# Rotary half-embedding: splitting the first load 4 + 12 rows and issuing tile 2's second half at a point of tile 1's arithmetic

## The chip, the cores and the metric

One core of one Trainium2 chip. The metric is the device time of one execution in microseconds; medians are over the executions of a run. There is only one core, so there are no other cores or dies to compare with; the granted clock was 1.0.

## The reference

`x` is 16 x 512 x 16 x 64 in fp32 (33.5 MB). The first half of the last axis is rotated with tables of cosines and sines, one row per position; the second half is copied.

```
x1, x2 = x[..., :32], x[..., 32:]
first  = x1[..., :16] * cos - x1[..., 16:] * sin      # cos, sin: first 16 columns, by position
second = x1[..., :16] * sin + x1[..., 16:] * cos
out    = concatenate([first, second, x2], axis=-1)
```

Every byte is read once and written once, 67.1 MB in all.

## The kernel before

Four tiles of 128 partitions x 16 rows (64 KB per partition, 8.4 MB each) go through three slots in SBUF. The rotation is in place on VectorE (DVE), eight rows at a time.

```python
ring = const_pool.tile([P, NS, K, H, D], fp32)         # NS = 3 slots, K = 16 rows, KC = 8, KM = 13
...
nc.gpsimd.dma_start(out=spread[:, 0, 0], in_=cosf)     # the two tables, on GpSimd's queue
nc.gpsimd.dma_start(out=spread[:, 0, 1], in_=sinf)
load(0)                                                # loads and stores: the sync engine's queue
load(1)
load(2, 0, KC)                                         # tile 2, first half
...                                                    # tables spread to all partitions
rotate(0, 0, KC)                                       # four VectorE instructions each
rotate(0, KC, K)
store(0)
load(2, KC, K)                                         # tile 2, second half, right behind store 0
load(3)                                                # slot of tile 0: waits until store 0 has landed
rotate(1, 0, KC)
rotate(1, KC, K)
behind_loads = store(1)                                # held until rotate(2, KC, KM) is done
rotate(2, 0, KC)
near = rotate(2, KC, KM)
rotate(2, KM, K)
store(2, queue=nc.gpsimd)
...
rotate(3, 0, KC)
rotate(3, KC, K)
store(3)
```

The sync engine works through its list in order: a transfer that has to wait holds up those written after it.

Of the kernel before, what the change touches and what calls it, by code (L numbers as in the profile page):

```python
# [1 line left out]

# [4 lines left out]


@with_exitstack
def kernel(  # L10
    ctx: ExitStack,
    tc: tile.TileContext,
    x: bass.AP,
    cos: bass.AP,
    sin: bass.AP,
    out: bass.AP,
):
    nc = tc.nc
    fp32 = mybir.dt.float32
    P = 128  # L20
    B, S, H, D = x.shape
    Q = D // 4
    HF = D // 2



    K = 16
    T = B * S // (P * K)
    PB = S // K
    REP = P // PB  # L30
    R = H * D
    NS = 3
    KC = K // 2
    KM = 13

    xf = x.rearrange("b s h d -> (b s h d)").rearrange("(t p f) -> t p f", t=T, p=P)
    of = out.rearrange("b s h d -> (b s h d)").rearrange("(t p f) -> t p f", t=T, p=P)
    cosf = cos.rearrange("(p k) j -> p (k j)", k=K)
    sinf = sin.rearrange("(p k) j -> p (k j)", k=K)

    const_pool = ctx.enter_context(tc.tile_pool(name="const", bufs=1))
    b_pool = ctx.enter_context(tc.tile_pool(name="bp", bufs=1, space=bass.MemoryType.PSUM))


    ring = const_pool.tile([P, NS, K, H, D], fp32)
    stage = const_pool.tile([P, 2, K, HF], fp32)
    spun = const_pool.tile([P, 2 * K, Q], fp32)
    packed = const_pool.tile([PB, 2 * K, Q], fp32)
    table = const_pool.tile([P, 2, K, 2, Q], fp32)

    def rows(t, lo, hi):
        return ring[:, t % NS, lo:hi].rearrange("p k h d -> p (k h d)")

    def load(t, lo=0, hi=K):
        return nc.sync.dma_start(out=rows(t, lo, hi), in_=xf[t, :, lo * R : hi * R])

    def store(t, lo=0, hi=K, queue=nc.sync):
        return queue.dma_start(out=of[t, :, lo * R : hi * R], in_=rows(t, lo, hi))  # L58


    nc.vector.memset(stage[:, :, :, 0:Q], 0.0)  # L61
    spread = stage.rearrange("(j b) t k i -> j b t (k i)", b=REP)
    nc.gpsimd.dma_start(out=spread[:, 0, 0], in_=cosf)  # L63
    nc.gpsimd.dma_start(out=spread[:, 0, 1], in_=sinf)  # L64
    load(0)
    load(1)
    load(2, 0, KC)




    PQ = PB // REP
    nc.vector.stream_shuffle(  # L73
        out=spun[:],
        in_=stage.rearrange("p t k j -> p (t k) j")[:, :, 0:Q],
        mask=[j % PQ * REP for j in range(PB)],
    )
    for q in reversed(range(REP)):
        n = PQ * (q + 1)
        nc.vector.tensor_copy(out=packed[0:n], in_=spun[q * PB : q * PB + n])  # L80

    for r in range(REP):
        nc.vector.tensor_copy(  # L83
            out=table[r * PB : (r + 1) * PB].rearrange("p t k c j -> p (t k) c j"),
            in_=packed.unsqueeze(2).to_broadcast((PB, 2 * K, 2, Q)),
        )
    C = table[:, 0].rearrange("p k c j -> p k (c j)")
    Sn = table[:, 1].rearrange("p k c j -> p k (c j)")

    def rotate(t, lo, hi):  # L90
        x1 = ring[:, t % NS, lo:hi, :, 0:HF]
        c = C[:, lo:hi].unsqueeze(2).to_broadcast((P, hi - lo, H, HF))
        s = Sn[:, lo:hi].unsqueeze(2).to_broadcast((P, hi - lo, H, HF))
        b_full = b_pool.tile([P, KC, H, HF], fp32, name="b_t")
        b_t = b_full[:, 0 : hi - lo]
        nc.vector.tensor_mul(out=b_t, in0=x1, in1=s)  # L96
        nc.vector.tensor_mul(out=x1, in0=x1, in1=c)  # L97
        nc.vector.tensor_sub(  # L98
            out=x1[:, :, :, 0:Q], in0=x1[:, :, :, 0:Q], in1=b_t[:, :, :, Q:HF]
        )  # L100
        return nc.vector.tensor_add(  # L101
            out=x1[:, :, :, Q:HF], in0=x1[:, :, :, Q:HF], in1=b_t[:, :, :, 0:Q]
        )

    rotate(0, 0, KC)
    rotate(0, KC, K)
    store(0)
    load(2, KC, K)
    load(3)
    rotate(1, 0, KC)  # L110
    rotate(1, KC, K)
    behind_loads = store(1)
    rotate(2, 0, KC)
    near = rotate(2, KC, KM)
    rotate(2, KM, K)
    store(2, queue=nc.gpsimd)

    tc.add_manual_dep(
        behind_loads.ins,
        near.ins.name,  # L120
        mybir.DependencyInfo(mybir.DependencyClass.Sync, mybir.DependencyReason.DATA),
        reason="the store follows the loads at the DMA engines",
    )
    rotate(3, 0, KC)
    rotate(3, KC, K)
    store(3)


# [1 line left out]
_INS = ['x', 'cos', 'sin']  # L130
_OUTS = [((16, 512, 16, 64), 'float32')]


# [23 lines left out]
```

## Time and profile before

| | before |
|---|---|
| time, median of the first 3 executions | 161.46 us (161.22 to 161.59) |
| span of the profiled execution | 159.5 us |
| bytes moved | 67.24 MB |
| VectorE busy | 112.9 us, 71% |
| DMA queues, share of 16 engines | 85.7% + 12.4% |
| first packet, last packet's end | 1.74 us, 158.2 us |

A profile of a kernel like this is read from the transfers, not from the engines: the DMA row and the queue table say that the sixteen DMA engines are at work for 98% of the span, and the trace's packet records (one start, duration and size per packet) say how well they work.

### The profile page before, as it was taken

The page shows a single profiled execution, that of the slowest core. Times are in us where ns is not written, and L with a number is a line of the kernel's source. Part 1 is how long each engine was busy: PE and PEld are TensorE (multiplying, and loading weights), DVE is VectorE, ACT ScalarE, POOL GpSimd, SP SyncE. Part 2 cuts the span into 40 slices and gives each one's busy share as a digit, 9 for nine tenths or more (in the row PEclk, how much of TensorE's full clock was granted, in tenths as well). Part 3 has the DMA queues.
Part 4 walks back from the last instruction along what each step waited for, and adds up shares of the span by engine and source line. Part 5 has one row for each costly group of instructions (what it writes and reads, how often), then busy time and mean ns, then how long its engine had stood idle before and what let it go on. Part 6 is the DMA issues. An engine that isn't in the chain of part 4 may idle for free.

```text
span 159.5 us, 115 instructions
## 1 busy us (share of the span) xinstructions
DVE 112.9 (71%) x47; POOL 1.9 (1%) x7
## 2 busy tenths in 40 slices
DVE  1000959999999999999999999999999990000000
POOL 3000000000000000000000000010000000000000
DMA  7969979899699699699996996996996996998966
GB/s 263 542 263 542 444 345 526 362 427 526 271 493 551 263 526 526 263 395 427 493 526 263 526 526 263 526 526 263 526 526 263 526 510 279 526 427 362 526 263 263
DMA packets 1360, 67.24 MB, mean 422 GB/s; under 512 B 176, under 2 KB 176, under 8 KB 208
## 3 DMA queue, kind: packets, MB, share of 16 engines
q1 hardware_dynamic: 1152, 58.72, 85.7%
q0 software_dynamic: 208, 8.52, 12.4%
HBM read 33.69 MB, written 33.55 MB: 422 GB/s over the span
## 4 chain that ended last, share of the span: by engine, by line
DVE 61%; DMA 14%; issue 5%; DVEq 1%
DVE b_t L96 22%; DVE ring L97 22%; DMA ring<-in_x_dram 14%; DVE ring L101 10%; DVE ring L98 7%; DVEq L152 1%; DVEq L96 0%
## 5 line engine op out<-in xcount | busy, mean ns | idle before, releaser
L96 DVE TENSOR_TENSOR b_t<-ring,table 128x4096 f32<-128x4096 f32 (+2 forms) x9 | 35.6, 3959 | 2.1 <-DMA ring<-in_x_dram 1.9
L97 DVE TENSOR_TENSOR ring<-ring,table 128x4096 f32<-128x4096 f32 (+2 forms) x9 | 35.6, 3950 | 0.3
L98 DVE TENSOR_TENSOR ring<-ring,b_t 128x2048 f32<-128x2048 f32 (+2 forms) x9 | 18.4, 2050 | 0.3
L101 DVE TENSOR_TENSOR ring<-ring,b_t 128x2048 f32<-128x2048 f32 (+2 forms) x9 | 18.4, 2043 | 0.0
L73 DVE LOAD_MASK_SELECT spun<-stage x1 | 0.0, 14 | 14.4 <-DMA stage<-in_sin_dram 14.4
L83 DVE COPY table<-packed 32x1024 f32<-32x1024 f32 x4 | 2.7, 684 | 0.1
L58 POOL DMA_DIRECT2D out_dram<-ring x1 | 0.6, 559 | 101.7 <-DVE ring L101 101.7
L80 DVE COPY packed<-spun 32x512 f32<-32x512 f32 (+3 forms) x4 | 1.7, 416 | 0.1
L61 DVE MEMSET stage<- 128x512 f32 x1 | 0.5, 485 | 0.9 <-PEq L141 0.9
L73 DVE STREAM_SHUFFLE spun<-stage 128x512 f32<-128x512 f32 x1 | 0.7, 722 | 0.0
L63 POOL DMA_DIRECT2D stage<-in_cos_dram x1 | 0.6, 642 | 1.3 <-DVE stage L61 1.3
L64 POOL DMA_DIRECT2D stage<-in_sin_dram x1 | 0.5, 532 | 0.0
L141 POOL MEMSET const-bfloat16-1.0<- 128x1 bf16 x1 | 0.1, 101 | 0.0
L141 POOL MEMSET const-float32-0.0<- 128x1 f32 x1 | 0.1, 98 | 0.2 <-issue 0.2
L141 POOL MEMSET const-float32-1.0<- 128x1 f32 x1 | 0.1, 98 | 0.0
L141 POOL MEMSET const-uint8-127<- 128x1 uint8 x1 | 0.1, 98 | 0.0
## 6 DMA issues: line engine op xcount, KB each, us to landing
ring<-in_x_dram SPq DMA_DIRECT2D x2, 4096.0 KB, 40.7
stage<-in_cos_dram POOLq DMA_DIRECT2D x1, 64.0 KB, 8.9
stage<-in_sin_dram POOLq DMA_DIRECT2D x1, 64.0 KB, 13.3
ring<-in_x_dram SPq DMA_DIRECT2D x3, 28.9
out_dram<-ring SPq DMA_DIRECT2D x3, 27.4
out_dram<-ring POOLq DMA_DIRECT2D x1, 39.5
```

The costliest lines, as they stand in the source:

```text
L58: return queue.dma_start(out=of[t, :, lo * R : hi * R], in_=rows(t, lo, hi))
L61: nc.vector.memset(stage[:, :, :, 0:Q], 0.0)
L63: nc.gpsimd.dma_start(out=spread[:, 0, 0], in_=cosf)
L64: nc.gpsimd.dma_start(out=spread[:, 0, 1], in_=sinf)
L73: nc.vector.stream_shuffle(out=spun[:], in_=stage.rearrange("p t k j -> p (t k) j")[:, :, 0:Q], mask=[j % PQ * REP for j in range(PB)],)
L80: nc.vector.tensor_copy(out=packed[0:n], in_=spun[q * PB : q * PB + n])
L83: nc.vector.tensor_copy(out=table[r * PB : (r + 1) * PB].rearrange("p t k c j -> p (t k) c j"), in_=packed.unsqueeze(2).to_broadcast((PB, ...
L96: nc.vector.tensor_mul(out=b_t, in0=x1, in1=s)
L97: nc.vector.tensor_mul(out=x1, in0=x1, in1=c)
L98: nc.vector.tensor_sub(out=x1[:, :, :, 0:Q], in0=x1[:, :, :, 0:Q], in1=b_t[:, :, :, Q:HF])
L101: return nc.vector.tensor_add(out=x1[:, :, :, Q:HF], in0=x1[:, :, :, Q:HF], in1=b_t[:, :, :, 0:Q])
L152: with _tile.TileContext(nc) as tc:
```

## The change

Its intent, by the text of the change: let the first rows come in as a small transfer of their own, and issue tile 2's second half "near the end of the one in front of it", as was done before for store 1 only.

```diff
-    load(0)
+    load(0, 0, KC // 2)
+    load(0, KC // 2, K)
     load(1)
     load(2, 0, KC)
...
     store(0)
-    load(2, KC, K)
+    rest = load(2, KC, K)
     load(3)
     rotate(1, 0, KC)
-    rotate(1, KC, K)
+    behind(rest, rotate(1, KC, K)[0])       # [0]: the first multiplication of that rotation
```

`rotate` now returns its first and last instruction, and `behind(transfer, point)` adds the dependence that store 1 had already. Nothing else moves.

More of the change, by code (lines that the diff above doesn't have):

```diff
@@ L95, in rotate @@
         b_t = b_full[:, 0 : hi - lo]
-        nc.vector.tensor_mul(out=b_t, in0=x1, in1=s)
+        begun = nc.vector.tensor_mul(out=b_t, in0=x1, in1=s)
         nc.vector.tensor_mul(out=x1, in0=x1, in1=c)
@@ L100, in rotate, with behind @@
         )
-        return nc.vector.tensor_add(
+        done = nc.vector.tensor_add(
             out=x1[:, :, :, Q:HF], in0=x1[:, :, :, Q:HF], in1=b_t[:, :, :, 0:Q]
+        )
+        return begun, done
+    def behind(transfer, point):
+        tc.add_manual_dep(
+            transfer.ins,
+            point.ins.name,
+            mybir.DependencyInfo(
+                mybir.DependencyClass.Sync, mybir.DependencyReason.DATA
+            ),
+            reason="issue the transfer near the end of the one in front of it",
         )
@@ L107 @@
     store(0)
-    load(2, KC, K)
+    rest = load(2, KC, K)
     load(3)
     rotate(1, 0, KC)
-    rotate(1, KC, K)
-    behind_loads = store(1)
+    behind(rest, rotate(1, KC, K)[0])
+    last = store(1)
     rotate(2, 0, KC)
-    near = rotate(2, KC, KM)
+    behind(last, rotate(2, KC, KM)[1])
     rotate(2, KM, K)
     store(2, queue=nc.gpsimd)
-    tc.add_manual_dep(
-        behind_loads.ins,
-        near.ins.name,
-        mybir.DependencyInfo(mybir.DependencyClass.Sync, mybir.DependencyReason.DATA),
-        reason="the store follows the loads at the DMA engines",
-    )
     rotate(3, 0, KC)
```

## The prediction

> **What bounds the kernel now.** I read the page first: the engines' busy shares, the DMA row of the forty slices, the queue table.
>
> ```profile
> DVE 112.9 (71%) x47; POOL 1.9 (1%) x7
> ...
> DMA  7969979899699699699996996996996996998966
> ...
> DMA packets 1360, 67.24 MB, mean 422 GB/s; under 512 B 176, under 2 KB 176, under 8 KB 208
> ...
> q1 hardware_dynamic: 1152, 58.72, 85.7%
> q0 software_dynamic: 208, 8.52, 12.4%
> ```
>
> VectorE (DVE) is busy for 71% of the span; the two DMA queues together for 85.7 + 12.4 = 98.1% of what sixteen engines could be. So the transfers bound the kernel. The 9-6-9 ripple is no idle time: a slice is 4 us, a packet is 64 KB and takes 2.4 us, and a packet is booked in one slice. Wider stretches, cut at the events of the queue, smooth it (columns: length, VectorE, GpSimd, clock, DMA share, GB/s):
>
> ```profile
> 0.00:1.74 1.74, 0.48 (x1) 0.24 (x5) 1.00 0.00 0
> ...
> 51.03:71.25 20.22, 20.08 (x6) 0.00 (x0) 1.00 1.03 439
> 71.25:99.85 28.60, 28.32 (x12) 0.00 (x0) 1.00 0.98 423
> 99.85:131.20 31.35, 31.04 (x12) 0.56 (x1) 1.00 1.00 435
> 131.20:158.20 27.00, 0.00 (x0) 0.00 (x0) 1.00 0.99 427
> 158.20:159.47 1.27, 0.00 (x0) 0.00 (x0) 1.00 0.00 0
> ```
>
> Nothing moves in the first 1.74 us and the last 1.27 us; between them the rate hardly leaves 430 GB/s, even after VectorE has finished at 131.2.
>
> The page's chain of waits says "DVE 61%; DMA 14%". That is a trap: it ends at the instruction that released the last store, and does not see that this store then stood in line behind another. So I went one level down, to the trace's packet records (start, duration, bytes), sorted by start into waves of sixteen, one packet per engine. They show one queue without a gap: 896 packets of 64 KB (56 waves, 2.418 us each at the median), 256 of 32 KB (16 waves of 1.213 us) and 32 table packets of 4 KB (2 waves of 0.159 us). At that pace: 56 x 2.418 + 16 x 1.213 + 2 x 0.159 = 155.1 us. From first packet to last end they took 158.22 - 1.74 = 156.5 us. **Only 1.3 us of 159.5 is lost inside the stream.** I find it in these places:
> - Wave 0, the first packets of all: 2.886 to 3.452 us each, mean 3.18, so about **0.75 us** over the pace. The engines start spread over 0.43 us.
> - Wave 31, the last packets of the first store, just ahead of tile 2's second half: those that began first took up to 3.318 us, those that began last 2.418. The latest end of the wave comes 81.73 - 78.93 = 2.80 us after that of the wave before, so about **0.38 us** over the pace.
> - The rest is some 5 ns per wave where stores run, and the spread at start and end.
>
> Last, the instruction timeline and the waits of the issuing queue:
>
> ```profile
> 0.74 1.33 SPq L55 DMA_DIRECT2D ring<-in_x_dram  x3
> ...
> 15.78 0.01 DVE L73 LOAD_MASK_SELECT spun<-stage  x1 [14.38 <-DMA stage<-in_sin_dram]
> ...
> 22.99 4.43 DVE L96 TENSOR_TENSOR b_t<-ring,table 128x4096 f32<-128x4096 f32 x1 [1.85 <-DMA ring<-in_x_dram]
> ...
> 49.87 0.35 SPq L58 DMA_DIRECT2D out_dram<-ring  x1
> ...
> 50.26 21.82 SPq L55 DMA_DIRECT2D ring<-in_x_dram  x2
> ```
>
> VectorE starts the rotation when tile 0 has landed (22.99), not when the tables are ready (1.85 us earlier), and then runs without a stop until 131.2. Its instructions therefore sit at fixed distances from the landing of tile 0, and release the transfers: store 0 at 49.87, store 1 at 98.86, store 3 at 131.2.
>
> **What the Trainium skill says.** "DMA: Bandwidth & Descriptors", section "Where 436 GB/s comes from", puts the ceiling of a core's sixteen engines at 435 GB/s. The trace agrees: 65,536 bytes in 2.418 us on 16 engines is 434 GB/s. There is no faster pace to be had. The same page, "Queues, rings and completion order", says that an engine takes turns between queues at packet granularity. The trace agrees: each table packet waited for a 64 KB packet's end, two tables were staged at 8.9 and 13.3 us after issue, and store 2 on the other queue alternates with store 1 from its second half on. "Perfetto Trace Analysis", section "DMA Optimizations", says that splitting helps when engines are generally idle; here they are not, which speaks against much gain.
>
> **The change, part by part.**
> 1. Load 0 in 4 and 12 rows: packets of 16 KB and 48 KB in place of 64 KB. From the two sizes measured, a packet costs about 8 ns plus 36.8 ns per KB (2 x 1.213 - 2.418 = 0.008). Estimates: 0.61 us for 16 KB and 1.81 for 48 KB, so eight more packets per engine add 8 x 8 ns = 0.06 us. One more issue on the queue (0.38 to 0.43 us) is paid while packets flow. The first rotation takes rows 0 to 8, so it now waits for both parts: **VectorE does not start on the first four rows.** The tables come sooner, because their packets wait for 0.6 us packets and not 2.4 us ones; from 15.8 us perhaps to 6 or 8. That adds slack to a wait that does not end last. What is left to win is wave 0's 0.75 us. If that is the latency of the first read, it stays whatever the size. If it scales with what is first asked of the memory, most goes. I choose a third: 0.25 - 0.06, about 0.2 us off.
> 2. Tile 2's second half waits for the first multiplication of tile 1's second half, which ended at 67.77. It is issued there and not at 50.26, 17.5 us later. In the order of each engine nothing changes: in the same queue it still follows store 0. Is there a gap? Issue to first packet was 1.74 - 0.74 = 1.0 us at the start, so its packets are ready by 68.8. The first engine finishes store 0 at about 70.7: **1.9 us of margin**. Load 3 behind it waits for store 0's landing at 71.8 either way. It can win wave 31's 0.38 us if the stretch comes from the load's reads starting under the last store packets; but by 68.8 that load is queued again, inside wave 31. I choose a third: 0.13 us off.
> 3. All arithmetic, tiles, bytes and the tail are unchanged. Store 0 keeps its place: issued 26.9 us after tile 0 lands, 1.15 us before its first packet at 51.03.
>
> The sum is 0.2 + 0.1 = 0.3 us, from 161.46 to about **161.1 us**. Removing both losses would give 161.46 - 0.75 - 0.38 = 160.3.
>
> **The rivals.**
> - The split exposes the start. If the first part's 16 KB packets ran out before the second part's descriptors are there, the engines would idle. Against it: eight packets of 0.61 us last 4.9 us, and issues follow each other at some 0.43 us. Cost if it is so: under 0.5 us.
> - The late issue opens a gap. If a wait on VectorE and an issue took 3 us and not 1.0, the engines would idle 1 us: 162.5. Against it: store 1 already works so, issued at 98.86 with its first packet at 99.85 and no gap.
> - VectorE becomes the bound, because it could start early on four rows. It cannot, and store 3 released at 131.2 had other packets ahead of it until its own first at 136.2.
> - The slow wave 0 and wave 31 are both caused by how transfers stand in the queue, and both vanish: 160.3. For it: somebody chose just these two places, and store 1, issued late, shows no stretch. Against it: store 1 follows a load, and the load-to-store change at store 0 shows none either.
>
> **Range and chances.** The most that can be won is 1.1 us, 0.7%, and 2% would be 3.2 us, more than all DMA idle time at both ends. So "faster" could only come from an error of measurement: 0.01. A gap of over 3.2 us needs two of the costs above at once: 0.01. The runs before spread over 0.37 us. The range 160.4 to 161.7 holds nearly the whole gain at one end and a small gap at the other.
>
> **What would show it.** Right: the first packets at 1.7 us; the table copies early but the first multiplication still started by the load, at 22.5 to 23.0; tile 2's second half issued near 67.5, with DMA share near 1 there; the last store issued near 131. The stretch in wave 31 tells part 2, the first waves part 1. Wrong if the first multiplication moves by over 0.7 us, if the DMA share dips near 70, or if the pace of 2.418 us itself changes.

## The result, and the profile after

The changed kernel takes **162.04 us** at the median (161.83 to 162.47, six executions), the kernel before 161.44 us in the same rounds (161.22 to 161.62). The ratio is 1.0038 with a 95% interval of 1.0023 to 1.0054. Ratios here and below are the mean time of one kernel's fast executions over that of the other's in the same rounds, so not quite the ratio of the medians that are quoted. Executions over 1.5% slower than the fastest of the same kernel are left out of the means. It is slower, clear of the noise, where 0.3 us of gain was forecast.

The page of the changed kernel, the same lines as before:

```profile
DVE 112.9 (71%) x47; POOL 1.9 (1%) x7
...
DMA  6999999969799799699999998997996996996990
...
DMA packets 1504, 67.24 MB, mean 420 GB/s; under 512 B 192, under 2 KB 192, under 8 KB 224
...
q1 hardware_dynamic: 1296, 58.72, 85.5%
q0 software_dynamic: 208, 8.52, 12.3%
```

Almost nothing to see: the same work, 144 packets more (128 data packets and 16 completions of the added transfer), 0.3 points less of the span. The instruction timeline shows the two moves as forecast:

```profile
0.74 1.95 SPq L55 DMA_DIRECT2D ring<-in_x_dram  x4
...
10.08 0.01 DVE L74 LOAD_MASK_SELECT spun<-stage  x1 [8.68 <-DMA stage<-in_sin_dram]
...
22.94 4.43 DVE L97 TENSOR_TENSOR b_t<-ring,table 128x4096 f32<-128x4096 f32 x1 [7.50 <-DMA ring<-in_x_dram]
...
49.82 0.35 SPq L58 DMA_DIRECT2D out_dram<-ring  x1
...
67.73 4.23 SPq L55 DMA_DIRECT2D ring<-in_x_dram  x2
```

The tables land 5.7 us sooner (10.08 for 15.78, where VectorE takes them up), VectorE starts 0.05 us sooner (22.94 for 22.99, still on the load), store 0 is issued 0.05 us sooner, and tile 2's second half is issued at 67.73. So far this is a small gain. The loss shows in the landings. In the next two fences, the first line of a pair is the issue (line, queue, transfer, count; its duration in ns; when it was issued), the second the time from issue to landing in us; the first pair is tile 2's second half, the second the last store. First the kernel before:

```profile
L55 SPq DMA_DIRECT2D ring<-in_x_dram x1: 433/433/433, 50.3 to 50.3; - x1
DMA to landing us min/median/max: 31.1/31.1/31.1
...
L58 SPq DMA_DIRECT2D out_dram<-ring x1: 344/344/344, 131.2 to 131.2; - x1
DMA to landing us min/median/max: 27.4/27.4/27.4
```

and the changed kernel:

```profile
L55 SPq DMA_DIRECT2D ring<-in_x_dram x1: 328/328/328, 67.7 to 67.7; - x1
DMA to landing us min/median/max: 14.0/14.0/14.0
...
L58 SPq DMA_DIRECT2D out_dram<-ring x1: 344/344/344, 131.1 to 131.1; - x1
DMA to landing us min/median/max: 27.8/27.8/27.8
```

Tile 2's second half lands at 50.3 + 31.1 = 81.4 us before and at 67.7 + 14.0 = 81.7 us after. The last store lands at 158.6 and at 158.9. The loss of 0.3 us is there when tile 2's second half lands, and it is carried to the end unchanged.

**Sixteen engines instead of one stream.** The view that explains it is not on the page. I followed the packet records engine by engine: on one engine a packet starts when the one before it ends, so each packet of 4 KB or more was given to the engine whose last packet ended nearest to its start (within 16 ns; every packet found a place). Engines have no names in this trace, and where one idles it could be swapped for another, but the extremes stand. For each engine I then took what it loses against the median pace of each packet size (2.418 us for 64 KB, 1.815 for 48, 1.213 for 32, 0.611 for 16), first in the load of tile 0, then at the turn from store 0 to tile 2's second half (store 0's last packet, the idle time behind it, the load's first three packets):

```
                       before     changed kernel
tile 0, mean of 16     0.77 us    0.64 us
the turn, mean of 16   0.39 us    0.50 us
the turn, worst        0.91 us    0.93 us
end, mean of 16      158.03 us  158.05 us
end, last of 16      158.21 us  158.59 us
```

The engines of the changed kernel end at the same time as before **in the mean**; the last of them ends 0.38 us later. Before, the last engine is 0.19 us behind the mean, afterwards 0.53 us. In the changed kernel the engine that ends last lost 0.93 us at the turn: it was 0.14 us behind the mean ahead of store 0, 0.05 us when store 0 ended, 0.55 us when tile 2's second half ended, and 0.53 us at the end. In the kernel before, the engine that lost 0.91 us at the turn was the first to begin its last store packet, and so came out only 0.19 us behind the mean.

Why a lag lasts: the Trainium skill, "DMA: Bandwidth & Descriptors", section "Why a DMA increments its semaphore by 16 and not by 1", says that each participating engine reports its own share, and that only the full sixteen mean that all data has landed. This trace agrees: every transfer has sixteen landings, and each engine has an equal share of each transfer (eight packets of each load or store). In these traces a late engine is not relieved by an early one, and no queue runs dry in which it could catch up. So the end of the stream is **the mean engine's end plus the lag of the last engine**, where the lag of an engine is how far it is behind the mean of the sixteen.

### The profile page after: what moved, and what is told of

It reads as the page before. It is cut to its first block, busy times and chain, and to the rows that moved or that the text cites. A ratio compares the mean times of both kernels' runs of the same rounds, so it can differ in the third digit from the quotient of the medians.

```text
span 160.0 us, 116 instructions
## 1 busy us (share of the span) xinstructions
DVE 112.9 (71%) x47; POOL 1.9 (1%) x7
## 4 chain that ended last, share of the span: by engine, by line
DVE 61%; DMA 14%; issue 5%; DVEq 1%; SPq 0%
DVE b_t L97 22%; DVE ring L98 22%; DMA ring<-in_x_dram 14%; DVE ring L102 10%; DVE ring L99 7%; DVEq L159 1%; SPq L55 0%; DVEq L97 0%
```

## The experiments

All kernels gave the correct result. "Turn" is always the one from store 0 to tile 2's second half. Diffs are against the kernel before, unless said. The time of the kernel before is that of the same rounds. The theories have the numbers that the expectations use:

- 1: the late issue of tile 2's second half costs (1a: through its short lead; 1b: through any issue during the store). 2: the split costs. 3: load 3's issue falls on the late load's first packets.
- 4: VectorE's start slips behind two landings. 5: an engine falls behind among the small packets. 6: any further transfer ahead of the turn costs. 7: small packets at the very start cost. 8: load 3's issue at the turn makes engines idle. 9: a store that is queued early behind a load costs.
- 10: the first load in two parts costs, in any order. 11: the tables' early packets do it. 12: the longer list of waits on store 0 does it.

### Each part alone

The split alone:

```diff
-    load(0)
+    load(0, 0, KC // 2)
+    load(0, KC // 2, K)
```

> The kernel before with only the first load split in 4 and 12 rows. If the late issue of tile 2's second half is what costs (theory 1), this run is 0.0 to 0.2 us faster than before (161.3 of 161.44), with the stretch in the last packets of store 0 as before. If the split is what costs (theory 2), it is about 0.6 us slower (162.0).

Measured: 161.18 to 163.84 us, median 162.55 (the slow one included) against 161.53; ratio of the fast executions 1.0044 (1.0005 to 1.0084). Neither theory had foreseen the spread. The profiled execution was the quick one: 161.18 us, with all sixteen engines within 0.27 us at the end. Its mean loss in tile 0's load was 0.52 us, a quarter of a microsecond less than before. So the split gained what was forecast in this one execution; the other four quick ones of both its runs took 161.46 to 161.57 us, as the kernel before.

The late issue alone:

```diff
-    load(2, KC, K)
+    rest = load(2, KC, K)
...
-    rotate(1, KC, K)
+    behind(rest, rotate(1, KC, K)[0])
```

> The kernel before with only tile 2's second half issued after the first multiplication of tile 1's second half. Theory 1 (the late issue costs): 0.5 to 0.8 us slower than before (about 162.1), and the first two waves of that load's packets stretched from 1.21 us to 1.4 to 2.1 us. Theory 2 (the split costs): as before, 161.4.

Measured: 161.75 us (161.25 to 162.14) against 161.53; ratio 1.0013 (0.9998 to 1.0027). The first theory, that this is where the loss is, falls: of the expected 0.5 to 0.8 us there is at most 0.4. But the waves look as that theory said. The mean over the engines at the turn:

```
                store 0's last packet   idle    load's first three packets   sum
before                0.35 us          0.01            0.03                 0.39 us
late_only             0.07 us          0.01            0.29                 0.37 us
```

The late issue takes the stretch away from the store's last packet and puts it into the load's first ones. The sum stays. This profile is the quickest of the six executions; the two at 162.01 and 162.14 us were not profiled, so it can't show what made them slower.

The same with more lead: the wait moved to the last addition of tile 1's first half.

```diff
+    behind(rest, rotate(1, 0, KC)[1])
```

> As late_only, but issued after the last addition of tile 1's first half, at about 63.3 us and not 67.8: some 7 us and not 2.6 us ahead of its first packet. If a short lead is what costs (theory 1a), most of the loss is gone: within 0.2 us of before, and first packets of 1.21 us. If any issue in mid-store costs (1b), it is as slow as late_only.

Measured: 161.64 us (161.26 to 161.79) against 161.53, ratio 0.9998 (0.9985 to 1.0011). No difference to the kernel before, as 1a said; but 1a's reason is not borne out, since late_only itself is not clearly slower. Its stretch is back in the store's last packet (0.66 us in the mean), as in the kernel before.

The late issue, and load 3 later still (`behind(third, rotate(1, KC, K)[1])`):

> late_only with load 3 also held, to the end of tile 1's arithmetic (about 76.8 us and not 71.7), which the queue can bear, because tile 2's second half lasts until 81. If the loss comes from load 3's issue falling on the late load's first packets (theory 3), the second wave's stretch goes and the time is back near before, 161.4 to 161.6. If it comes from the late load's own start (theory 1), it stays at 162.0 or more.

Measured: 161.56 us (161.44 to 161.80) against 161.53, ratio 1.0002 (0.9990 to 1.0014). Back near before, as theory 3 has it, but the difference to late_only is within the spread, and the stretch in the load's first packets is still there (0.27 us). This decides nothing about load 3; split_l3_76 below does.

### Catching a slow execution of the split

> split_only gave 161.2 to 163.8 us in six executions, and its profile caught a quick one. Two more looks, to catch a slow one. If VectorE's start slips because both landings are awaited (theory 4), a slow execution has its first multiplication over 23.2 us, store 0 issued as much later than 49.9 us, and an idle stretch of the engines ahead of store 0. If an engine falls behind among the small packets (theory 5), the waves of load 0 spread by over 1 us with store 0 still at 49.9 us.

> The same kernel as split_look_a, a second chance of catching an execution over 162 us. Theory 4: VectorE starts late and store 0 follows a gap. Theory 5: the waves of load 0 spread between engines, and the gap is on one or two engines only.

Measured: 163.49 and 162.33 us in one execution each (state unknown, as for any single look; split_only has fast executions at 162.5 to 163.55). In the slow one VectorE's first multiplication starts at 22.99 us and store 0 is issued at 49.87 us, exactly as in the kernel before. Theory 4, the wait for two landings, is dead. So is theory 5 as I had put it: the waves of tile 0's load are not torn apart. The difference is at the turn. Tile 2's second half and the last store in the slow look:

```profile
L55 SPq DMA_DIRECT2D ring<-in_x_dram x1: 432/432/432, 50.3 to 50.3; - x1
DMA to landing us min/median/max: 32.4/32.4/32.4
...
L58 SPq DMA_DIRECT2D out_dram<-ring x1: 343/343/343, 131.2 to 131.2; - x1
DMA to landing us min/median/max: 29.3/29.3/29.3
```

Issued at the same 50.3 us as before, it lands 1.3 us later (32.4 for 31.1); the last store lands 1.9 us later. The engines show who it is:

```
                     before   split_look_a   split_look_b
turn, mean of 16     0.39     0.61           0.46   us
turn, worst three    0.91     1.40           1.32
                     0.64     1.27           0.80
                     0.63     0.84           0.58
end, mean of 16    158.03   158.27         157.99
end, last of 16    158.21   160.13         158.84
```

Two engines, and in the second look one, lose 1.3 to 1.4 us; each of them stood idle for 0.5 to 0.7 us between the last packet of store 0 and the first of the load, which had been in the queue for some 20 us. The others are as ever. In the first look the two engines that end last lost another 0.42 and 0.56 us at the turn from load 3 to store 1.

### The changed kernel again, and the parts in another order

> The changed kernel once more, beside the split alone: 161.9 to 162.3 us, less spread (0.6 us) than the split alone (2.7 us).

Measured: 161.94 to 163.26 us, median 162.47 (four executions) against 161.58, ratio 1.0059 (1.0022 to 1.0095). The spread is 1.3 us, not 0.6, so the changed kernel spreads as the split alone does. Its profile shows the mean engine at 158.14 us and the last at 158.71.

The first load in 12 and 4 rows:

```diff
-    load(0)
+    load(0, 0, 12)
+    load(0, 12, K)
```

> The first load in 12 and 4 rows: two transfers as in split_only, but the first packets are of 48 KB. If the small packets at the very start cost (theory 5), it is back at 161.4 to 161.6 us with little spread. If it is the wait for two landings (theory 4), it spreads as split_only does, 161.2 to 163.8.

Measured: 162.68 us (162.53 to 162.89), ratio 1.0072 (1.0055 to 1.0089). Neither expectation. I had overlooked that the first eight rows lie within the first twelve, so that VectorE could start at 18.19 us, and store 0 was issued at 45.07 us, 6.9 us before its first packet (the next expectation says 5.6). The last two packets of the load in front of it took 1.06 us too long in the mean, and the turn behind store 0 was free. So this run moved two things and says nothing about small packets; that a store which is queued early behind a load costs (theory 9) is only a guess from it.

Store 0 held back in that kernel (`first = store(0)`, `behind(first, rotate(1, 0, KC)[0])`):

> split_12_4 with store 0 held from 45.1 to about 49.5 us. In split_12_4 store 0 was queued 5.6 us ahead of its first packet and the last two packets of the load in front took 1.06 us too long in the mean over the engines. If that comes from queuing a store early behind a load (theory 9), most of 1 us comes back: 161.5 to 162.0 of 162.7. If it does not, it stays at 162.5 or more.

Measured: 163.91 us, ratio 1.0155 (1.0142 to 1.0169). I had put the point of issue at 49.5 us; it was 51.16, and the engines stood still for some 0.8 us ahead of store 0. They lost another 0.8 us at the turn and 1.3 us at the turn to store 1. The run misses its purpose, and theory 9 stays open. With store 0 held, the load in front of it lost nothing; but in both kernels store 1 was also queued early behind load 3, by 6.3 us in split_12_4 and 6.5 us here, and load 3's last packets lost 0.14 us in the mean there and 1.26 us here.

### What it is not: one more transfer, or load 3

Tile 1's load in two parts, the first load whole:

```diff
-    load(1)
+    load(1, 0, KC // 2)
+    load(1, KC // 2, K)
```

> Tile 1's load in 4 and 12 rows, the first load whole. If one more transfer ahead of the turn from store 0 to tile 2's second half is what makes that turn lose more on single engines (theory 6), this run spreads as split_only does, 161.2 to 163.8 us with a mean over 162. If it is the small packets at the very start (theory 7), it stays at 161.4 to 161.8.

Measured: 161.73 us (161.38 to 161.79) against 161.43, ratio 1.0011 (0.9998 to 1.0024); the last engine 0.16 us behind the mean. One more transfer ahead of the turn does not do it. It matters that it is the first load.

The split with load 3 held to 76.8 us (`behind(third, rotate(1, KC, K)[1])`):

> split_only with load 3 held to the end of tile 1's arithmetic, 76.8 us and not 71.7. The slow looks of split_only showed one or two engines idle for 0.5 to 0.65 us just where load 3 was issued, ahead of tile 2's second half. If load 3's issue at the turn is what makes them idle (theory 8), the spread collapses to 161.2 to 161.7 us. If not, it stays at 161.2 to 163.8.

Measured: 162.36 us (161.43 to 162.61), ratio 1.0046 (1.0025 to 1.0066), and in its profile two engines lose 1.4 us at the turn although load 3 was not issued before 76 us. They did not stand idle (0.05 us at most): their last packets of store 0 and first packets of the load took too long. So load 3's issue is not what costs, and standing idle is only one form of the loss. Theory 8 falls.

The changed kernel with load 3 held in the same way:

> The changed kernel with load 3 held to 76.8 us. Theory 8: 161.2 to 161.6, as quick as before or quicker, because the split's 0.1 to 0.2 us at the start is kept. Otherwise: 161.9 to 162.5 as the changed kernel.

Measured: 161.88 us (161.60 to 162.03) against 161.43, ratio 1.0025 (1.0013 to 1.0037). Theory 8 wanted it back at the time of the kernel before, and it is not.

### Two parts in any order and size

Rows 4 to 16 first, rows 0 to 4 last:

```diff
-    load(0)
+    load(0, KC // 2, K)
+    load(0, 0, KC // 2)
```

> The same two parts of the first load in the other order: rows 4 to 16 first (48 KB packets), rows 0 to 4 last (16 KB). VectorE still waits for both and starts at about 22.9 us, and the number of transfers is that of split_only. If small packets at the very start are what lets single engines lose 1.3 us at the turn (theory 7), the spread is gone: 161.3 to 161.8 us. If it is the first load in two parts, whatever the order (theory 10), it spreads as split_only, 161.2 to 163.8.

Measured: 163.26 us (163.14 to 163.61) against 161.54, ratio 1.0109 (1.0096 to 1.0122). Slower in all four executions. VectorE starts at 23.10 us, and the first packets are of 48 KB, so small first packets are not needed: theory 7 falls. At the turn two engines lost 1.8 and 2.0 us. The arrival of the tables, VectorE's start, and the landings of tile 2's second half and of the last store:

```profile
14.20 0.01 DVE L74 LOAD_MASK_SELECT spun<-stage  x1 [12.80 <-DMA stage<-in_sin_dram]
...
23.10 4.43 DVE L97 TENSOR_TENSOR b_t<-ring,table 128x4096 f32<-128x4096 f32 x1 [3.54 <-DMA ring<-in_x_dram]
...
L55 SPq DMA_DIRECT2D ring<-in_x_dram x1: 433/433/433, 50.4 to 50.4; - x1
DMA to landing us min/median/max: 32.5/32.5/32.5
...
L58 SPq DMA_DIRECT2D out_dram<-ring x1: 344/344/344, 131.3 to 131.3; - x1
DMA to landing us min/median/max: 29.0/29.0/29.0
```

Two halves of eight rows (`load(0, KC, K)`, `load(0, 0, KC)`):

> The first load in two halves of 8 rows (32 KB packets), the half that VectorE needs last, so that it starts at about 22.9 us. Theory 7 (small first packets): between before and split_only, under 162. Theory 10 (two parts): as split_only, a median over 162 and a spread over 1 us.

Measured: 161.76 us at the median with 161.44 to 163.10, ratio 1.0024 (0.9997 to 1.0051). The spread is there (1.7 us), the median over 162 is not, so this lies between. In the profiled execution some waves of tile 1's load were slow on all engines alike (about 2.5 us for 2.418), and the turn cost next to nothing (0.01 us in the mean).

Four parts of four rows, the first four rows last (`for lo in (4, 8, 12, 0): load(0, lo, lo + 4)`):

> The first load in four parts of 4 rows, all 16 KB packets, the first four rows last, VectorE at about 22.9 us. Theory 7 or 10: spread as split_only or wider, median over 162. If the effect needs the change of packet size within the first load (16 to 48 KB), it is near before, under 161.8.

Measured: 162.64 us (162.28 to 163.81), ratio 1.0075 (1.0050 to 1.0099). A change of packet size within the first load is not needed either.

> split_only beside the three above on the same chip: a median of 161.5 to 162.6 and a spread over 1 us, as in its eight executions so far.

Measured: 161.84 us (161.46 to 162.87), ratio 1.0022 (0.9997 to 1.0047); the profiled execution (162.66 us) has one engine with a loss of 1.6 us at the turn. Over both runs, seven of twelve timed executions of the split alone lie above 161.9 us (one of the seven is slow); none of the 57 executions of the kernel before does (of late_only, two of six do).

### Two last differences

An extra wait on store 0, in the kernel before:

```diff
-    nc.gpsimd.dma_start(out=spread[:, 0, 0], in_=cosf)
+    cos_load = nc.gpsimd.dma_start(out=spread[:, 0, 0], in_=cosf)
...
+    tc.add_manual_dep(first.ins, cos_load.ins.name, ...)     # first = store(0)
```

> The kernel before, the first load whole, with one more wait on store 0, on the long landed table of cosines: with the split, store 0 waits for two landings and not one. If the longer list of waits at store 0's issue is what leads to the spread (theory 12), this run spreads as split_only does, with a median over 161.8. If it is the packets of the split load, it is as before, 161.3 to 161.7.

Measured: 161.67 us (161.55 to 161.71), ratio 1.0013 (0.9999 to 1.0028). No spread: theory 12 falls.

The split, with fills on GpSimd that were to delay the tables:

> split_only with some 5 us of idle fills on GpSimd ahead of the two table loads, so that the tables land at about 14 to 16 us as in the kernel before and not at 10. VectorE still starts when tile 0 has landed. If the tables' early packets among the small ones are what leads to the spread (theory 11), the run is back at 161.3 to 161.8 us. If not, it keeps a median over 161.8 and a spread over 1 us.

Measured: 163.02 us (161.55 to 163.80), ratio 1.0095 (1.0059 to 1.0132). But the scheduler put only three of the ten fills ahead of the tables, and VectorE had them at 9.98 us, as early as in the split alone. The experiment did not make the change that it was meant to test. It is one more case of the spread (one engine with a loss of 1.6 us at the turn), and says nothing of theory 11, the early tables. Another run does: in split_rev VectorE had the tables only at 14.20 us, inside the 14 to 16 us that were wanted here, and two engines lost 1.8 and 2.0 us all the same. Early tables are not needed for the loss.

### All profiles in one table

The mean engine and the last engine, from the profiled execution of each kernel:

```
kernel              that execution   end, mean of 16   end, last   last - mean   turn, worst engine
before                  161.40 us        158.03          158.21       0.19           0.91
two_waits               161.55           158.06          158.22       0.17           0.79
split_tile1             161.66           158.11          158.27       0.16           0.89
late_only               161.25           157.98          158.11       0.12           0.72
late_63                 161.79           158.42          158.58       0.16           1.12
late_l3_76              161.56           158.07          158.37       0.30           0.99
changed kernel          162.13           158.05          158.59       0.53           0.93
after_again             162.15           158.14          158.71       0.57           0.54
after_l3_76             162.03           158.22          158.88       0.67           1.10
split_only              161.18           157.81          157.99       0.18           0.67
split_only_again        162.66           158.05          159.21       1.17           1.63
split_look_b            162.33           157.99          158.84       0.85           1.32
split_look_a            163.49           158.27          160.13       1.86           1.40
split_l3_76             162.23           158.05          159.06       1.01           1.41
split_tables_late       162.81           158.00          159.26       1.25           1.57
split_4x4               162.28           158.20          158.86       0.66           1.03
split_rev               163.28           158.45          159.96       1.51           2.04
split_rev_8             161.99           158.20          158.43       0.23           0.11
split_12_4              162.53           158.78          159.16       0.37           0.03
```

The rows of late_63, split_rev and split_12_4 say that the mean can move too, by some 0.4 to 0.75 us; but what sets the split apart is the fifth column. With the first load whole, the last engine is 0.12 to 0.30 us behind the mean. With the load split it is 0.5 to 1.9 us behind in ten of thirteen profiles, the changed kernel's among them; split_only's quick execution, split_rev_8 and split_12_4, with 0.2 to 0.4 us, are the exceptions. (split_12_4_hold, with its gap, is left out of the table.) One execution stands for each kernel here; those with the first load whole took 161.25 to 161.79 us, so none of their slowest is among them.

## Why the prediction was wrong

The bound was read rightly: the transfers, not VectorE, and no part of the change altered that. The forecast of the mechanics was right as well: VectorE did not start on the first four rows, the tables came sooner to no effect, the late issue opened no gap, and the last store was issued at 131.1 us. What failed are the two terms of the sum, and a term that was not in it.

**Part 1, "about 0.2 us off".** The gain is there, but smaller. Against the pace of each packet size, the mean loss in the load of tile 0 fell from 0.77 to 0.64 us (0.52 in the split alone), and the eight further packets cost their 0.06 us: the mean engine ended that load at 22.22 us for 22.29, so 0.07 us net and not 0.2. Of the two cases that the prediction left open, the traces favour the first, a latency that stays whatever the size: in all these profiles the first packet of an engine took, in the mean, 0.61 to 0.76 us over the pace with 64, 48 or 32 KB, and still 0.38 to 0.65 us (0.59 in the changed kernel) with 16 KB.

**The step that failed** is "The sum is 0.2 + 0.1": it adds means over the engines, as if the mean engine set the end, and has no term for the lag of single engines. In the changed kernel's profile that term is 0.53 - 0.19 = 0.34 us, which together with 0.02 us of the mean makes up the 0.38 us (with rounding) by which the last packet ends later, out of the 0.5 us between the spans. The rest, about 0.1 us, comes after the last packet.

**Part 2, "0.13 us off".** The cause that I named, the load's reads starting under the last store packets, fits what happened: with the late issue the store's last packets are no longer stretched. But the cost moved to the load's own first packets, and 0.39 us became 0.37 with the late issue alone and 0.50 in the changed kernel. So nothing was won here; the late issue alone gave a ratio of 1.0013 with an interval that includes 1.

**The rival that was nearest** was the fourth, that both slow places come from how transfers stand in the queue. It had the place and the wrong sign. The rivals named with a loss, an exposed start and a gap at the late issue, did not occur.

**Readings in the prediction to put right.** The ends of waves at 81.73 and 78.93 are counted from the start of the trace, 10.48 us before that of the span; on the clock of all other times they are 71.25 and 68.45, at the end of store 0. The 36.8 ns are per 1000 bytes; per KB of 1024 bytes it is 37.7, with which the estimates of 0.61 and 1.81 us were worked, and these were borne out (0.611 and 1.815). VectorE had the tables at 10.08 us and not at "6 or 8".

**The range.** The upper end of 161.7 was set by the spread of the kernel before, 0.37 us. The changed kernel has a spread of its own, 161.83 to 163.26 us over ten executions. A forecast from one profile of one kernel could not know it, but the profile held the warning: wave 0 and wave 31 were shown engine by engine, from 2.886 to 3.452 us and from 2.418 to 3.318, and I then worked on with their means.

**Settled and open.** Shown: the loss is a lag of one or two engines. In eight of the ten profiles in which the last engine ends 0.5 us or more behind, its lag can be followed and grows at the turn from store 0 to tile 2's second half, in the changed kernel from 0.05 to 0.55 us, in split_only_again from 0.41 to 1.18 us. The split of the first load brings such a lag, in most executions, in either order and in the sizes tried (five of twelve executions of the split alone are as quick as the kernel before, and split_rev_8 lies between).

Not shown: why splitting the first load makes an engine lose time at that turn, some 50 us after the load has landed. In five profiles the engine stands idle for 0.5 to 1.6 us, in others its packets there take too long. VectorE's start, the number of transfers, load 3's issue, the waits on store 0, small packets at the start and early tables are excluded as sole causes. One rival was not tested: ahead of store 0 the sixteen engines are nearer in step where the first load begins with 16 KB packets (their ends lie within 0.28 to 0.50 us, with the first load whole within 0.46 to 0.97). But in split_rev they lie within 0.55 us, as in the kernel before with 0.52, and two engines fell far behind.

Not shown either: that the late issue has no part in it. Its own profile shows no lag, but is its quickest execution. And the changed kernel was never as quick as the kernel before in ten executions (161.83 us at least), the split alone in five of twelve; what the two do together was not separated.

One thing is only an observation: in the three profiles in which store 0 was issued 1.8 us or more before its first packet (after_again, split_rev_8, split_12_4) the turn cost 0.14 us or less in the mean, and in the others, with 0.8 to 1.4 us, it cost 0.3 to 0.8 us. It is no recipe: in these three the loads behind tile 0's had already lost 0.50, 0.67 and about 1.0 us over the pace, in the others 0.04 at most, and their mean engine ended no earlier than before. I found no version that beats the kernel before; late_63 and late_l3_76 equal it.

## What to carry to other kernels

Where a kernel keeps sixteen DMA engines busy from first to last, as this one does, its end is the mean engine's end plus the lag of the last one; read the packets per engine, not per wave, before forecasting a change in the order or size of transfers. The stretch at the change from a store to a load was not won here by moving the moment of issue: look where such a cost goes. And time such changes in several executions, for a change can leave the best case as it was, or better it, and still lose through its spread.

## What the Trainium skill lacked or had wrong

- No page has a cost for the change from stores to loads in one queue. "DMA: Bandwidth & Descriptors" is where it belongs: 0.3 to 0.8 us per engine in the mean in most of these profiles, up to 2.04 us on one engine, at a point where the queue was never empty.
- "DMA: Bandwidth & Descriptors", "Why a DMA increments its semaphore by 16 and not by 1", explains the sixteen reports, but not that with a full queue the lag of one engine outlasts the transfer. Here, in split_only_again, the last engine was 1.18 us behind the mean at the end of tile 2's second half and 1.17 us at the end of the kernel.
- "Perfetto Trace Analysis", "DMA Optimizations", advises splitting where engines are idle, and has no figure for what it costs where they are not. Here splitting the first of five loads into two cost 0.2 to 0.4% in the mean (the 0.2% with an interval that includes zero) and raised the spread from 0.3 to 0.4 us to 1.4 and 2.7 us; splitting the second load the same way cost nothing that could be measured (1.0011, 0.9998 to 1.0024).
- "DMA: Bandwidth & Descriptors", "Latency and other measured facts", gives a first-byte latency of some 600 ns for this queue. It does not say from where it counts: from the start of the first issue to the first packet record the trace before shows 1.0 us, and from the end of that issue, which took 0.38 us, some 0.6 us, which agrees. What the page lacks is that the first packets of the kernel before then take 0.5 to 1.0 us longer than the later ones.
